# Pairs of heads that enter the shared buffers in three parts, with token-shift sums and chain steps issued later, in a streaming encoder layer on one core

## The chip, the cores and the metric

The kernel runs on one core of a Trainium2 chip. A core has a matrix engine (TensorE, PE in the profile; its weight loads are PEld), a vector engine (VectorE, DVE), a scalar engine (ScalarE, ACT), a general engine (GpSimd, POOL) and a sync engine (SyncE, SP), which here only issues DMAs. Each engine works through its own queue strictly in order, and engines wait for one another by semaphores. Matmuls write to PSUM, a small accumulator memory that DVE and ACT read and POOL does not; everything else lies in SBUF.

The metric is the device time of one execution in microseconds (us), as the median of several runs.

## The reference, cut to what matters

One layer: a projection of 1024 prompt rows and 64 sample rows, a gated-MLP half A and an RWKV-7 half B of 16 heads, and an output projection that sums both halves.

```python
z = h @ w_in                                     # (1024 + 64) x 2048 @ 2048 x 7296
za, zs, g_b = split(z)
u, v, g_a = split(za)
out_a = gelu(u) * sgu_mix(layer_norm(gelu(v)), w_s, b_s) * silu(g_a)

zs_mix = zs + mu * (previous_row(zs) - zs)       # token shift
r, k, vb, hw, ha = split(zs_mix)
decay = exp(-exp(-softplus(-(w0 + tanh(hw) @ w2)) - 0.5)); a = sigmoid(a0 + ha @ a2)
kk = normalise(k * k_k); k = k * (1 + (a - 1) * k_a)
for t in range(T):                               # per head, state S is 64 x 64
    S = S * w_t + (-S @ kk_t) (kk_t * a_t)^T + v_t k_t^T
    y_t = S @ r_t
y = group_norm(y) + (sum(r * k * r_k)) * v
out_b = y * silu(g_b)
o = concat([out_a, out_b]) @ w_out
y_out = rms_norm(x + o)
```

## The kernel before

**Order of the work.** The program is written by a planner in Python (class `Builder`): it emits instructions in one fixed order for each engine and keeps rough clocks (`self.clk`) only to decide what to emit next. The main line in `run` goes through the 57 blocks of `w_in` (128 columns each), then through `w_out` in two halves of eight weight groups (half 0 multiplies the first eight 128-row pieces of the concatenation, half 1 the others). A block of the projection is three groups of tokens (364, 364, 360); each group is 48 matmuls into one of two PSUM tiles `mp`. Values are split into two float16 parts, so each product takes three matmuls. After every second matmul the main line calls `poll`, which lets the generators in `self.side` emit a piece of other work when the time that they yielded has come on PE's clock.

**Side work.** Each weight block is prepared by `wprep` (ACT squares and casts, DVE forms the low part `w<-raw,sci,w`). Blocks 24 to 48 are token-shifted by `z_mix`: ACT evicts `mp` (and one last column, `zc` or `sht`), then DVE adds the shifted part straight from PSUM (`u<-mp,zs,u`).

**Pairs.** The 16 heads of half B go in eight pairs, each cut into 17 chunks of 64 rows (chunk 16 is the sample). `front(q)` makes the inputs of pair q; its elementwise products of 128x1088 run on POOL (`tt` with `eng=nc.gpsimd`). Then it copies them into the shared buffers `AR` and `KB`, in parts given by `PARTS`; a part of pair q may enter when pair q-1 has passed a flag (`mid` after chunk 7, `chain` at its end). `wkv(q)` forms the chunk products, inverts 32x32 triangles by a forward substitution of 60 DVE instructions (`u<-u`, `u<-u,u`), and then runs the chain over the chunks: matmul `yps<-S,wk`, DVE add `wk<-yps,wk`, matmul `smp<-wk`, DVE update `S<-S,pc,smp`, and again. After each half step it yields the time at which the DVE result is planned to be ready, plus `slack`. PE is in order, so a chain matmul that comes before its DVE result is ready stops the main line behind it.

**PSUM.** Side work shares two tiles `bigp` and two `smp`. `room(tags)` yields until the planner thinks that the next tiles have been read; `lora`, `head_sums` and `post` take tiles without it.

**Between the projections.** `mix_prep(0)` casts the eight pieces of half 0 to two float16 parts (ACT `...,pwi 128x544`, then DVE `...,pwi,... 128x544`), after the flag `kbfree` of pair 7. Pieces go to free slots `u`, or, once the projection is through, to the freed buffer of h (`bigt`), from where `mix_move` takes them later. `acc_load` loads x into the accumulators of the output; group 0's load is issued by SP. `out_first` multiplies weight group 0 with pieces 0 to 5 of four row tiles, then 6 and 7, and `out_add` adds the result to x on DVE (`bigt<-mp,sc,bigt`), which frees the PSUM tile.

Of the kernel before, what the change touches and what calls it, by code (L numbers as in the profile page):

```python
# [39 lines left out]
TWO23 = 8388608.0  # L40
PARTS = ((0, 8), (8, 17))
RES = 2


class Builder:
# [101 lines left out]
    def add(self, gen, front=False, backlog=600):  # L147
        if front:
            self.side.insert(0, [0, gen, 1e9])
        else:  # L150
            self.side.append([0, gen, backlog])

    def poll(self):
        self.npoll += 1
        assert self.npoll < 60000, [(g.__name__, g.gi_frame.f_lineno) for _, g, _ in self.side]
        for it in list(self.side):
            if it[0] > self.now or self.clk[DV] > self.now + it[2]:
                continue
            try:
                w = next(it[1])  # L160
                it[0] = self.now + 400 if w is None else w
            except StopIteration:
                self.side.remove(it)
# [30 lines left out]

    def tt(self, out, a, b, op, eng=None, dep=None):
        (eng or self.nc.vector).tensor_tensor(out, a, b, op)  # L196
        if eng is not None:
            return self.fin(PO, 100 + self.width(out) * 2.2, dep)
        return self.read(a, self.fin(DV, 150 + self.width(out) / 0.96, dep))
# [362 lines left out]
    def in_group(self, blk, st, t0, n):  # L562
# [25 lines left out]
        if 24 <= blk < 49:  # L588
            self.zmix = self.z_mix(blk, ps, t0, n, inv)
            self.evt = next(self.zmix)  # L590
            self.add(self.zmix, front=True)
            return
        else:
            o, func = self.U(self.gelu_buf[blk])[:, t0:t0 + n], AF.Gelu if blk < 16 else AF.Silu
            if blk in self.late:
                func = AF.Copy
        self.evt = self.act(o, ps[:, 0:n], func, scale=inv)

    def z_mix(self, blk, ps, t0, n, inv):
        i, g = blk - 24, MG.index((t0, n))  # L600
        o, zs, zc = self.U(self.gelu_buf[blk]), self.zs[:, self.zi % 2], self.zc[:, self.zi % 2]
        last = g == 2
        m = NP - t0 if last else n
        f = self.act(o[:, t0:t0 + n], ps[:, 0:n], AF.Copy, scale=zs[:, 0:1])
        c = self.sh[:, 0, i:i + 1] if last else zc[:, g:g + 1]
        f = self.act(c, ps[:, m - 1:m], AF.Copy, scale=inv)
        if last:
            f = self.act(self.sh[:, 1, i:i + 1], ps[:, n - 1:n], AF.Copy, scale=inv)
        yield f
        f = self.stt(o[:, t0 + 1:t0 + m], ps[:, 0:m - 1], zs[:, 1:2], o[:, t0 + 1:t0 + m], ALU.mult, ALU.add)  # L610
        if g:
            f = self.stt(o[:, t0:t0 + 1], zc[:, g - 1:g], self.vcol(V_MU, i), o[:, t0:t0 + 1], ALU.mult, ALU.add)
        if last:
            self.stt(o[:, NP + 1:NT], ps[:, m:n - 1], zs[:, 1:2], o[:, NP + 1:NT], ALU.mult, ALU.add)
            f = self.tt(o[:, NP:NP + 1], o[:, NP:NP + 1], self.mst[:, i:i + 1], ALU.add)
            self.flags.add(("zm", blk))
        yield f
# [175 lines left out]
    def lora(self, half, hw, out, bias):  # L793
        for t0, n in TG:
            pt = self.bigt()
            for p in range(2):
# [5 lines left out]
    def head_sums(self, a, b=None):  # L802
        b = a if b is None else b
        pa, pb, ps = self.bigt(), self.bigt(), self.smt()
        for h in range(2):
            hp, br, one = HP[h], HP[1 - h], self.bones[HP[h], HP[h]]
            self.mm(pa[hp, :], one, a[hp, 0:512], cost=260)
            self.mm(pb[br, :], one, a[hp, 512:1024], cost=260)
        for hp in HP:
            self.mm(ps[hp, 0:64], self.bones[hp, hp], a[hp, NP:NT], cost=55)  # L810
        parts = [(slice(0, 128), slice(0, 512), pa[:])] + [(HP[h], slice(512, 1024), pb[HP[1 - h]]) for h in range(2)]
        parts.append((slice(0, 128), slice(NP, NT), ps[:, 0:64]))
        return [(a[p, c], i) if b is a else (a[p, c], i, b[p, c]) for p, c, i in parts]

    def front(self, q):
# [41 lines left out]
        yield self.act(SQ, K, AF.Square, scale=self.vcol(V_KK, q))  # L857
        for o, i in self.head_sums(SQ):
            f = self.act(o, i, AF.Ln)
        yield f - 300  # L860
# [25 lines left out]
        for part, (c0, c1) in enumerate(PARTS):  # L886
            if q > 0:
                yield from self.wait(("mid" if part == 0 else "chain", q - 1))
            if part == 0:
# [12 lines left out]
        yield from self.wait(("vt", q))  # L902
        for _, i, o in self.head_sums(R, V):
            f = self.tt(o, i, o, ALU.mult)
        yield f
# [6 lines left out]
    def wkv(self, q):  # L912
# [5 lines left out]
        pc = self.pc[q % 2]  # L918
        slack = 250 if q < 7 else 0
        mv = MK.rearrange("p (r c) g k -> p c r g k", r=2)  # L920
        KR, BR = HP, (HP[1], HP[0])
        def vtr(part):
            c0, c1 = PARTS[part]
            V = self.U(P["v"])
            for c in range(c0, c1, 8):
# [12 lines left out]
                yield f  # L938
            if part:
                self.flags.add(("vt", q))  # L940
        af = AR.rearrange("p c s t -> p c (s t)")
        def ktr(part):
            c0, c1 = PARTS[part]
            if part:
                yield from self.wait(("kt0", q))
            for c in range(c0, c1, 4):
# [6 lines left out]
                yield f  # L953
            self.flags.add(("kbfree" if part else "kt0", q))
        def atr():
# [140 lines left out]
        for c in [16] + list(range(16)):  # L1096
# [22 lines left out]
            if c == 16:  # L1119
                yield from self.room("big")  # L1120
                pt = self.bigt()
                for h, hp in enumerate(HP):
                    self.mm(pt[0:64, hp], MR[:, c, h, :], VS[:, c, hp], cost=60)
                self.tt(yd, pt[0:64, 0:128], yd, ALU.add)
            elif c % 8 == 7:
                yield from self.room("big")
                pt = self.bigt()
                for i in range(4):
                    for h, hp in enumerate(HP):
                        for d in range(2):  # L1130
                            cc = c - 7 + 2 * i + d
                            self.mm(pt[HP[d], i * 128 + h * 64:i * 128 + h * 64 + 64], MR[:, cc, h, :], VS[:, cc, hp],
                                    cost=60)
                y = Y[:, c // 2 - 3:c // 2 + 1, :]
                self.tt(y, pt[:].rearrange("p (i f) -> p i f", f=128), y, ALU.add)
            if c == 16:
# [5 lines left out]
            else:  # L1142
                S = Sn
            if c == PARTS[0][1] - 1:
                self.flags.add(("mid", q))
            yield f + slack
# [31 lines left out]
    def post(self, q):  # L1178
# [15 lines left out]
        gg = self.vcol(V_GG, q)  # L1194
        for i in (0, 4):
            pt = self.bigt()
            for r in range(4):
                self.tr(pt[:, r * 128:(r + 1) * 128], YN[:, i + r].rearrange("p h f -> p (h f)"))
            c = slice(i * 128, i * 128 + 512)
            yield self.stt(BV[:, c], pt[:], gg, BV[:, c], ALU.mult, ALU.add)  # L1200
        pt = self.bigt()
        yield from self.wait(("yns", q))
        self.tr(pt[:, 0:64], self.yns[HP[q % 2]], 64, HP[q % 2])
# [185 lines left out]
    def acc_load(self):  # L1389
        nc = self.nc  # L1390
        self.accs = self.big[:, 16384:17408].rearrange("p (j t) -> p j t", t=64)
        for g in range(8):
            if g == 1:
                yield from self.wait(("mixT", 0))
            if g >= 4:
                yield from self.wait("moved")
            self.dma(nc.gpsimd if g else nc.sync, self.acc_view(g),
                     self.a["x"][0:NP, g * 256:(g + 1) * 256].rearrange("(t p) n -> p t n", p=128))
# [226 lines left out]
```

## Time and profile before

| | |
|---|---|
| median of 3 runs | 2029.97 us (2026.56 to 2030.69) |
| the profiled execution's own time | 2022.13 us |
| its span, first to last instruction | 2020.4 us |
| busy PE, DVE, ACT, POOL | 96%, 57%, 51%, 17% of the span |
| mean granted TensorE clock | 0.993 of full speed |

How to read it: PE is busy nearly all the time, so what can be won lies in the moments in which it is idle or runs at the lower clock, and each of them has a line and a cause in the trace. The profiled execution is 7.84 us (0.4%) below the median of the runs.

### The profile page before, as it was taken

What the parts mean: (1) busy time and instruction counts of PE and PEld (TensorE: products, weight loads), DVE (VectorE), ACT (ScalarE), POOL (GpSimd) and SP (SyncE); (2) the same over time, 40 slices, a digit from 0 to 9 for tenths busy, and PEclk for the clock granted to TensorE, in tenths of its full rate; (3) what the DMA queues carried; (4) which work ended last, traced back from release to release, by engine and by line L of the source; (5) the groups of instructions that cost most, each with busy time, mean ns of one, the idle gap of its engine ahead of it and who ended that gap; (6) DMA issues with size and microseconds to landing.
All of it is one profiled execution on the core that took longest, in us unless ns stands there. A gap on an engine that the chain in (4) does not pass through costs nothing.

```text
span 2020.4 us, 42834 instructions
## 1 busy us (share of the span) xinstructions
PE 1930.4 (96%) x18445; PEld 1393.1 (69%) x18445; DVE 1151.7 (57%) x2517; ACT 1026.6 (51%) x1834; POOL 339.7 (17%) x304
## 2 busy tenths in 40 slices
PE   6999999997999999899999989999999979999998
PEld 5966667665666666566666666666666658899997
DVE  6574684483475556647457565654754856533444
ACT  7633345555457455645655736755654542422433
POOL 2400002400410230240042022024004201000000
PEclk9999999999999999999999999999999989999999
DMA  6211124221212311322222222223122454412214
GB/s 234 95 64 42 66 81 158 92 66 60 89 61 96 110 62 54 108 105 70 88 90 67 99 94 74 88 76 118 39 98 99 151 191 130 167 43 89 80 34 146
DMA packets 52189, 190.65 MB, mean 94 GB/s; under 512 B 6880, under 2 KB 18672, under 8 KB 42336
## 3 DMA queue, kind: packets, MB, share of 16 engines
q1 hardware_dynamic: 42672, 156.71, 22.3%
q0 software_dynamic: 6880, 22.26, 3.2%
q10 hardware_dynamic: 2448, 8.94, 1.1%
q8 instruction: 145, 2.38, 0.5%
q14 instruction: 44, 0.36, 0.1%
HBM read 140.32 MB, written 45.93 MB: 92 GB/s over the span
## 4 chain that ended last, share of the span: by engine, by line
PE 82%; ACT 7%; DVE 7%; DMA 2%; issue 2%; SPq 0%; DVEq 0%; POOL 0%; ACTq 0%
PE mp L238 69%; PE bigp L238 7%; ACT u L184 3%; PE smp L238 2%; DVE w L192 2%; DVE u L192 2%; ACT L184 2%; PE bigp L243 1%; DVE u L196 1%; PE yps L238 1%; ACT w L184 1%; ACT wk L184 1%; DMA o_ss<-S 1%; DVE wk L196 1%; DVE S L1113 1%
## 5 line engine op out<-in xcount | busy, mean ns | idle before, releaser
L238 PE MATMUL mp<-bigt,w 128*128 128x364 f16 (+3 forms) x8514 | 1326.5, 310 | 4.3 <-DVE w L192 1.4
L238 PEld LDWEIGHTS <-w 128*128 128x128 f16 x9216 | 814.7, 98 | 410.2 <-issue 4.9
L192 DVE SCALAR_TENSOR_TENSOR w<-raw,sci,w 128x512 f16<-128x512 f32 x276 | 225.3, 841 | 186.8 <-ACT w L184 185.8
L238 PEld LDWEIGHTS <-wk 128*128 128x128 f16 x2304 | 210.4, 98 | 33.7 <-issue 10.2
L238 PE MATMUL mp<-w,wk 128*128 128x256 f16 x1728 | 204.3, 274 | 10.0 <-DVE bigt L192 10.0
L184 ACT ACTIVATE w<-raw,sci 128x512 f16<-128x512 f32 x276 | 186.3, 713 | 53.6 <-DVE sci L296 43.7
L196 POOL TENSOR_TENSOR u<-u,u 128x1088 f32<-128x1088 f32 x56 | 140.8, 2525 | 337.7 <-DVE u L192 129.1
L184 ACT ACTIVATE w<-raw 128x2048 bf16<-128x2048 f32 (+1 forms) x70 | 131.7, 1882 | 92.2 <-PE mp L238 85.9
L184 ACT ACTIVATE wk<-bigp 128x512 f32<-128x512 f32 (+5 forms) x240 | 120.1, 523 | 88.6 <-PE bigp L238 69.4
L184 ACT ACTIVATE u<-yps 64x128 f32<-64x128 f32 x120 | 32.7, 273 | 225.7 <-DVE wk L196 225.3
L184 ACT ACTIVATE u<-mp,sc 128x364 f32<-128x364 f32 (+3 forms) x109 | 57.0, 523 | 169.3 <-PE mp L238 168.7
L184 ACT ACT_TABLE_LOAD x95 | 121.9, 1283 | 35.0 <-PE bigp L238 19.1
L238 PE MATMUL mp<-w,u 128*128 128x256 f16 x1065 | 133.8, 276 | 3.4 <-DVE u L1039 2.9
L192 DVE SCALAR_TENSOR_TENSOR bigt<-mp,sc,bigt 128x512 f32<-128x512 f32 (+2 forms) x83 | 53.9, 652 | 130.5 <-PE mp L238 120.3
L238 PEld LDWEIGHTS <-u 128*128 128x128 f16 x1065 | 104.4, 99 | 18.6 <-DVE u L192 3.2
L196 POOL TENSOR_TENSOR wk<-wk,mask 128x512 f32<-128x512 f32 (+1 forms) x80 | 85.0, 1083 | 119.9 <-ACT wk L184 119.9
L1113 DVE SCALAR_TENSOR_TENSOR S<-S,pc,smp 64x64 f32<-64x64 f32 x240 | 66.8, 278 | 60.7 <-PE smp L238 52.5
L196 DVE TENSOR_TENSOR u<-u,u 128x30 f32<-128x30 f32 (+15 forms) x248 | 92.3, 372 | 8.3
L196 DVE TENSOR_TENSOR u<-bigp,u 128x512 f32<-128x512 f32 (+2 forms) x64 | 40.4, 632 | 92.1 <-PE bigp L238 90.8
L184 ACT ACTIVATE u<-mp,zs 128x364 f32<-128x364 f32 (+1 forms) x75 | 42.1, 561 | 96.1 <-PE mp L238 95.4
L192 DVE SCALAR_TENSOR_TENSOR u<-mp,zs,u 128x363 f32<-128x363 f32 (+1 forms) x100 | 49.5, 495 | 72.0 <-ACT zc L184 38.8
L238 PE MATMUL smp<-wk 64*64 64x64 f32 (+1 forms) x816 | 66.0, 239 | 21.4 <-DVE wk L196 19.9
(186 smaller groups left out, 1892.1 us busy)
## 6 DMA issues: line engine op xcount, KB each, us to landing
raw<-w_in SPq DMA_DIRECT2D x54, 1024.0 KB, 4.9
raw<-w_out SPq DMA_DIRECT2D x14, 1024.0 KB, 5.0
z_d<-u SPq DMA_DIRECT2D x24, 544.0 KB, 2.9
u<-z_d SPq DMA_DIRECT2D x24, 544.0 KB, 5.0
mix_d<-u ACTq DMA_DIRECT2D x16, 544.0 KB, 3.5
o_y<-bigt SPq DMA_DIRECT2D x16, 512.0 KB, 4.5
wk<-x SPq DMA_DIRECT2D x7, 1024.0 KB, 8.1
bigt<-x POOLq DMA_DIRECT2D x7, 1024.0 KB, 6.5
```

The source lines that it names most:

```text
L184: self.nc.scalar.activation(out, in_, func, bias=bias, scale=scale, **kw)
L192: self.nc.vector.scalar_tensor_tensor(out, in0, s, in1, op0, op1)
L196: (eng or self.nc.vector).tensor_tensor(out, a, b, op)
L238: self.nc.tensor.matmul(out, lhsT, rhs, start=start, stop=stop)
L243: self.nc.tensor.transpose(out, in_, self.ident[p, p])
L1113: self.nc.vector.scalar_tensor_tensor(Sn[hp, hp], Sc[hp, hp], pc[hp, c - 1:c], pu[hp, hp], ALU.mult, ALU.add)
```

## The change

Seven edits, of which the first six move instructions:

1. `PARTS` has three entries (chunks 0 to 7, 8 to 11, 12 to 16); the second may enter after chunk 11 of the pair before (flag `late`). The output sums of the chunks are made after chunks 7, 11 and 15, and those of chunk 16 by one 128x128 matmul and two adds in place of two matmuls and one add.
2. `z_mix` yields 800 ns more than the planned end of its eviction, and is put into `self.side` with that time, so that the sums are not emitted at the next poll but 800 ns after the planned eviction.
3. `slack` of the chain is 500 ns (250 before), still 0 for pair 7.
4. POOL's 128x1088 products are issued as two instructions.
5. `lora`, `head_sums` and `post` wait with `room` for tiles that are planned to have been read.
6. The load of x for group 0 is issued by ACT, not SP.
7. `HARD` in `poll` changes nothing (`w + 0`).

```diff
-PARTS = ((0, 8), (8, 17))
+PARTS = ((0, 8), (8, 12), (12, 17))
...
     def tt(self, out, a, b, op, eng=None, dep=None):
+        if eng is not None and self.width(out) == NT:
+            h = out.shape[1] // 2
+            for c in (slice(0, h), slice(h, out.shape[1])):
+                eng.tensor_tensor(out[:, c], a[:, c], b[:, c], op)
+            return self.fin(PO, 200 + NT * 2.2, dep)
...
             self.zmix = self.z_mix(blk, ps, t0, n, inv)
             self.evt = next(self.zmix)
-            self.add(self.zmix, front=True)
+            self.side.insert(0, [self.evt, self.zmix, 1e9])
...
-        yield f
+        yield f + 800
         f = self.stt(o[:, t0 + 1:t0 + m], ps[:, 0:m - 1], zs[:, 1:2], o[:, t0 + 1:t0 + m], ALU.mult, ALU.add)
...
     def lora(self, half, hw, out, bias):
         for t0, n in TG:
+            yield from self.room("big")
             pt = self.bigt()
...
+        yield from self.room("big", "big", "sm")
         pa, pb, ps = self.bigt(), self.bigt(), self.smt()
...
-                yield from self.wait(("mid" if part == 0 else "chain", q - 1))
+                yield from self.wait((("mid", "late", "chain")[part], q - 1))
...
-        slack = 250 if q < 7 else 0
+        slack = 500 if q < 7 else 0
...
-            elif c % 8 == 7:
+            elif c in (7, 11, 15):
+                m = 8 if c == 7 else 4
...
         for i in (0, 4):
+            yield from self.room("big")
             pt = self.bigt()
...
+        yield from self.wait(("yns", q))
+        yield from self.room("big")
         pt = self.bigt()
-        yield from self.wait(("yns", q))
...
-            self.dma(nc.gpsimd if g else nc.sync, self.acc_view(g),
+            self.dma(nc.gpsimd if g else nc.scalar, self.acc_view(g),
```

**Place one: DVE at the 36th of the 100 sums that read `mp`,** in the chain of pair 1. Before (`yps` is the chain's product, `S` its state, `sci` and `sc` belong to a weight block, `gst` to the group norm):

```order
L1113 SCALAR_TENSOR_TENSOR S_110<-S_109,pc_107,smp 64x64 x2
L295 TENSOR_SCALAR sci_116<-smp 128x1
L296 TENSOR_SCALAR sci_116<-sci_116 128x1
L298 TENSOR_SCALAR sc_113<-sci_116,kin 128x1
L220 RECIPROCAL gst<-gst 128x16
L192 SCALAR_TENSOR_TENSOR u_83<-mp,zs,u_83 128x363
L196 TENSOR_TENSOR wk<-yps,wk 64x128
```

The same sum in the changed kernel:

```order
L305 TENSOR_SCALAR sc_113<-sci_116,kin 128x1
L194 SCALAR_TENSOR_TENSOR u_90<-mp,zs,u_90 128x363
L1178 TENSOR_REDUCE gst<-u_84 128x16
L211 TENSOR_SCALAR gst<-gst 128x16
L194 SCALAR_TENSOR_TENSOR w_79<-raw,sci_116,w_78 128x512
L203 TENSOR_TENSOR u_84<-u_84,gst 128x1024
L203 TENSOR_TENSOR wk<-yps,wk 64x128
```

Before, the sum stands directly ahead of a chain add; now other work lies between them, and the chain of the pair begins later beside the main line. Over the whole program 42 of the 100 sums stand directly ahead of a chain instruction before, and 10 in the changed kernel.

**Place two: ACT from the last group of the input projection on.** Before (the 128x360 row is the last eviction of the projection; `...,pwi 128x544` are casts of half 0, two for each piece; the four pieces ahead of these rows are cast already):

```order
L184 ACTIVATE u_92<-mp,sc_113 128x360
L184 ACTIVATE w_79,sc_119<-raw 128x2048
L184 ACTIVATE u_91<-bigt,pwi 128x544 x2
L184 ACTIVATE bigt<-bigt,pwi 128x544
L184 ACTIVATE w_78<-raw,sci_116 128x512
L184 ACTIVATE bigt<-bigt,pwi 128x544 x5
L184 ACTIVATE wk<-u_90 32x8x2x32
```

The changed kernel:

```order
L186 ACTIVATE wk<-u_81,pwi 128x544
L186 ACTIVATE u_85<-mp,sc_113 128x360
L186 ACTIVATE w_79,sc_119<-raw 128x2048
L186 ACTIVATE wk<-u_81,pwi 128x544
L186 ACTIVATE wk<-u_86,pwi 128x544 x2
L186 ACTIVATE bigt<-u_87,pwi 128x544 x2
L186 ACTIVATE bigt<-bigt,pwi 128x544 x10
L186 ACTIVATE w_78<-raw,sci_116 128x512 x4
L253 DMA bigt<-x 128x8x256
```

Eight casts come after the last eviction before, fifteen now; the load of x stands behind them on ACT. Before it stood on SP, behind two loads of weights:

```order
L246 DMA bv_d<-u_92 128x1088
L246 DMA raw<-w_out 128x2048 x2
L246 DMA bigt<-x 128x8x256
L246 DMA g_d<-u_92 128x1088
```

**Place three: DVE in the changed kernel at the same point.** `u_88` and `u_83` are the forward substitution of pair 7:

```order
L194 SCALAR_TENSOR_TENSOR wk<-u_86,pwi,wk 128x544
L194 SCALAR_TENSOR_TENSOR bigt<-u_87,pwi,bigt 128x544 x2
L203 TENSOR_TENSOR u_83<-u_88 128x168
L203 TENSOR_TENSOR u_88<-u_88,u_83 128x24x7
L203 TENSOR_TENSOR u_83<-u_88 128x184
L203 TENSOR_TENSOR u_88<-u_88,u_83 128x23x8
L194 SCALAR_TENSOR_TENSOR bigt<-bigt,pwi 128x544 x4
L203 TENSOR_TENSOR u_83<-u_88 128x198
L203 TENSOR_TENSOR u_88<-u_88,u_83 128x22x9
L203 TENSOR_TENSOR u_83<-u_88 128x210
L203 TENSOR_TENSOR u_88<-u_88,u_83 128x21x10
L194 SCALAR_TENSOR_TENSOR bigt<-bigt,pwi 128x544 x4
```

Before, DVE has finished the 60 instructions of that substitution when it comes to the casts that follow the projection; now the casts lie in the middle of it.

## Rows read from the trace of the kernel before

**Rows 1.** Busy time by stage; columns: us, then PE, PEld, DVE, ACT, POOL, granted clock, DMA.

```profile
440.00:1606.00 1166.00, 1120.65 (x10555) 749.41 (x10553) 679.10 (x1547) 665.23 (x1163) 246.71 (x198) 1.00 0.24 85
1606.00:1666.00 60.00, 41.93 (x584) 32.90 (x582) 36.36 (x79) 25.30 (x44) 7.63 (x12) 0.86 0.60 208
...
sum 2020.40, PE 1930.38 PEld 1393.08 DVE 1151.74 ACT 1026.61 POOL 339.73; mean PE 386.08 PEld 278.62 DVE 230.35 ACT 205.32 POOL 67.95
```

**Rows 2.** What PE waited for, whole span: us in total, times, longest.

```profile
PE smp L238 <- DVE wk L196: 19.9, 13, 3.1
PE yps L238 <- DVE S L1113: 13.6, 14, 3.3
```

**Rows 3.** Timeline, stalls behind token-shift sums: start, us, engine, instruction, [idle before <-releaser].

```profile
490.98 0.79 PE L238 MATMUL smp<-wk 128*128 128x128 f32 x2 [2.76 <-DVE wk L196]
...
651.24 0.60 DVE L192 SCALAR_TENSOR_TENSOR u<-mp,zs,u 128x363 f32<-128x363 f32 x1 [3.52 <-ACT zc L184]
...
652.21 0.49 PE L238 MATMUL smp<-wk 128*128 128x128 f32 x2 [3.09 <-DVE wk L196]
...
1483.94 0.49 PE L238 MATMUL smp<-wk 128*128 128x128 f32 x2 [0.97 <-DVE wk L196]
```

**Rows 4.** Groups by line and shape: busy us, mean ns of one, idle before it.

```profile
L184 ACT ACTIVATE w<-raw 128x2048 bf16<-128x2048 f32 x68 | 129.6, 1907 | 91.9 <-PE mp L238 85.9 <-DMA raw<-w_in 5.9
...
L184 ACT ACTIVATE wk<-u,pwi 128x544 f16<-128x544 f32 x20 | 13.5, 734 | 3.4 <-DVE pwi L289 3.4
...
L196 POOL TENSOR_TENSOR u<-u,u 128x1088 f32<-128x1088 f32 x56 | 140.8, 2525 | 337.7 <-DVE u L192 129.1 <-DVE u L206 70.1 <-ACT w L184 56.3
...
L196 POOL TENSOR_TENSOR wk<-wk,pc 128x512 f32<-128x512 f32 x24 | 26.3, 1097 | 0.0
...
L192 DVE SCALAR_TENSOR_TENSOR wk<-u,pwi,wk 128x544 f16<-128x544 f32 x20 | 15.1, 779 | 6.3 <-ACT wk L184 6.3
...
L196 DVE TENSOR_TENSOR u<-u 128x240 f32<-128x240 f32 x16 | 6.5, 405 | 0.4
...
L192 DVE SCALAR_TENSOR_TENSOR w<-u,sci,w 128x512 f16<-128x512 f32 x8 | 5.6, 745 | 0.9 <-ACT w L184 0.9
```

**Rows 5.** Timeline, stalls while POOL runs its products.

```profile
503.19 0.49 PE L238 MATMUL smp<-wk 128*128 128x128 f32 x2 [1.14 <-DVE wk L196]
...
845.73 7.64 POOL L196 TENSOR_TENSOR u<-u,u 128x1088 f32<-128x1088 f32 x3 [1.50 <-DVE u L206]
...
849.04 4.88 DVE L192 SCALAR_TENSOR_TENSOR w<-raw,sci,w 128x512 f16<-128x512 f32 x2
...
854.28 0.49 PE L238 MATMUL smp<-wk 128*128 128x128 f32 x2 [2.59 <-DVE wk L196]
...
1504.37 0.49 PE L238 MATMUL yps<-S,wk 128*128 128x128 f32 x2 [0.57 <-DVE S L1113]
```

**Rows 6.** Timeline, a matmul that waits for its PSUM tile.

```profile
463.44 1.01 PE L238 MATMUL bigp<-u,lwh 128*128 128x512 f16 x2 [3.20 <-ACT wk L184]
```

**Rows 7.** The chain that ended last: a weight group of the output, start, us.

```profile
1747.73 22.38 PE mp L238 x240
```

**Rows 8.** Busy time and granted clock around the first pair's chain, columns as in rows 1.

```profile
454.50:505.00 50.50, 40.23 (x390) 26.49 (x391) 17.96 (x54) 27.83 (x51) 3.79 (x4) 0.93 0.17 60
```

**Rows 9.** Timeline from the last projection group to the second weight group of half 0.

```profile
1602.96 27.39 SPq L246 DMA_DIRECT2D raw<-w_out  x2
...
1610.66 0.32 PE L238 MATMUL mp<-bigt,w 128*128 128x360 f16 x1
...
1630.44 0.39 SPq L246 DMA_DIRECT2D bigt<-x  x1
...
1640.95 1.41 DVE L192 SCALAR_TENSOR_TENSOR bigt<-mp,sc,bigt 128x512 f32<-128x512 f32 x2 [9.76 <-DMA bigt<-x]
1641.75 1.44 PE L238 MATMUL mp<-w,wk 128*128 128x256 f16 x6 [7.76 <-DVE bigt L192]
...
1661.31 0.91 PE L238 MATMUL mp<-w,wk 128*128 128x256 f16 x4 [2.19 <-DVE bigt L192]
```

More of the change, by code (lines that the diff above doesn't have):

```diff
@@ L151, in add @@
             self.side.append([0, gen, backlog])
+    HARD = ("wkv", "startup")
     def poll(self):
@@ L160, in poll @@
                 w = next(it[1])
-                it[0] = self.now + 400 if w is None else w
+                it[0] = self.now + 400 if w is None else w if it[1].__name__ in self.HARD else w + 0
             except StopIteration:
@@ L806, in head_sums @@
             hp, br, one = HP[h], HP[1 - h], self.bones[HP[h], HP[h]]
-            self.mm(pa[hp, :], one, a[hp, 0:512], cost=260)
-            self.mm(pb[br, :], one, a[hp, 512:1024], cost=260)
+            self.mm(pa[hp, :], one, a[hp, 0:512], cost=230)
+            self.mm(pb[br, :], one, a[hp, 512:1024], cost=230)
         for hp in HP:
@@ L812, in head_sums @@
         parts.append((slice(0, 128), slice(NP, NT), ps[:, 0:64]))
-        return [(a[p, c], i) if b is a else (a[p, c], i, b[p, c]) for p, c, i in parts]
+        for p, c, i in parts:
+            yield a[p, c], i, b[p, c]
     def front(self, q):
@@ L857, in front @@
         yield self.act(SQ, K, AF.Square, scale=self.vcol(V_KK, q))
-        for o, i in self.head_sums(SQ):
-            f = self.act(o, i, AF.Ln)
+        for hs in self.head_sums(SQ):
+            if isinstance(hs, tuple):
+                f = self.act(hs[0], hs[1], AF.Ln)
+            else:
+                yield hs
         yield f - 300
@@ L902, in front @@
         yield from self.wait(("vt", q))
-        for _, i, o in self.head_sums(R, V):
-            f = self.tt(o, i, o, ALU.mult)
+        for hs in self.head_sums(R, V):
+            if isinstance(hs, tuple):
+                f = self.tt(hs[2], hs[1], hs[2], ALU.mult)
+            else:
+                yield hs
         yield f
@@ L938, in vtr @@
                 yield f
-            if part:
+            if part == 2:
                 self.flags.add(("vt", q))
@@ L944, in ktr @@
             if part:
-                yield from self.wait(("kt0", q))
+                yield from self.wait(("kt", q, part - 1))
             for c in range(c0, c1, 4):
@@ L953, in ktr @@
                 yield f
-            self.flags.add(("kbfree" if part else "kt0", q))
+            self.flags.add(("kt", q, part))
+            if part == 2:
+                self.flags.add(("kbfree", q))
         def atr():
@@ L1121, in wkv @@
                 pt = self.bigt()
-                for h, hp in enumerate(HP):
-                    self.mm(pt[0:64, hp], MR[:, c, h, :], VS[:, c, hp], cost=60)
-                self.tt(yd, pt[0:64, 0:128], yd, ALU.add)
-            elif c % 8 == 7:
+                self.mm(pt[:, 0:128], MR[:, c].rearrange("p g k -> p (g k)"), VS[:, c])
+                for hp in HP:
+                    self.tt(yd[:, hp], pt[hp, hp], yd[:, hp], ALU.add)
+            elif c in (7, 11, 15):
+                m = 8 if c == 7 else 4
                 yield from self.room("big")
                 pt = self.bigt()
-                for i in range(4):
+                for i in range(m // 2):
                     for h, hp in enumerate(HP):
                         for d in range(2):
-                            cc = c - 7 + 2 * i + d
+                            cc = c + 1 - m + 2 * i + d
                             self.mm(pt[HP[d], i * 128 + h * 64:i * 128 + h * 64 + 64], MR[:, cc, h, :], VS[:, cc, hp],
                                     cost=60)
-                y = Y[:, c // 2 - 3:c // 2 + 1, :]
-                self.tt(y, pt[:].rearrange("p (i f) -> p i f", f=128), y, ALU.add)
+                y = Y[:, (c + 1 - m) // 2:c // 2 + 1, :]
+                self.tt(y, pt[:, 0:m * 64].rearrange("p (i f) -> p i f", f=128), y, ALU.add)
             if c == 16:
@@ L1143, in wkv @@
                 S = Sn
-            if c == PARTS[0][1] - 1:
-                self.flags.add(("mid", q))
+            if c in (7, 11):
+                self.flags.add(("mid" if c == 7 else "late", q))
             yield f + slack
```

## Prediction

> **What bounds the kernel now.** I read first the busy times. PE works 1930.4 of the 2020.4 us span [rows 1], so 90 us of idle time, and the stretches in which its clock is low, are all that an edit of order can win. The busy time by stage says where they lie. The pairs' chains run beside the projection from 440 to 1606 us; there PE idles 1166.0 - 1120.65 = 45.35 us. The passage from the input to the output projection, 1606 to 1666 us, idles 18.07 us, at a granted clock of 0.86 of full speed [rows 1]. The remaining 27 us lie in the start and in the output stage, where the change moves nothing.
>
> Next come PE's waits. The two steps of the chain, `smp` waiting for DVE's add and `yps` waiting for DVE's state update, are 27 stalls and 33.5 us [rows 2], three quarters of the first figure. The length of each chain step is no trouble: a chain add takes some 0.28 us. So the timeline must tell why DVE is late. It shows two reasons, and a third that has to do with PSUM:
>
> - **Shift sums.** At 651.24 DVE has stood idle for 3.52 us at a token-shift sum whose input ACT has not yet evicted; the chain add is queued behind it, and PE stalls 3.09 us [rows 3]. Going through every stall, I count 10 that end behind such a sum, from 490.98 to 1483.94 us, 15.4 us in all.
> - **POOL.** Its 128x1088 products take 2.5 us each [rows 4]. While three of them run (845.73, 7.64 us), two DVE low parts take 4.88 us, where 0.745 us apiece is usual [rows 4, 5]; the chain step behind them comes 2.59 us late. I count 12 stalls of this kind, from 503.19 to 1504.37 us, 16.8 us in all.
> - **PSUM.** A product of `lora` waits 3.20 us for its tile, which ACT is still reading [rows 6]. With two smaller ones that is 5.2 us.
>
> What is left of the 45.35 us is 7.9 us in short pieces.
>
> **The change, part by part.** *The sums, 800 ns later and no longer at the head of the queue.* They are emitted when their eviction should be over, so DVE need not stand at them, and a chain add need not stand behind. Place one shows it: 42 of 100 sums stood directly ahead of a chain instruction, 10 do now. In proportion, 15.4 x 10/42 = 3.7 us stay; with the larger slack (next) I take 2. Bounds: nothing left, or half left (7.7) if the planner's time for the eviction is as far off as in [rows 3]. Gain 13.4 (7.7 to 15.4).
>
> *Slack 500 for 250 ns.* Each chain matmul is put a quarter of a microsecond further from its DVE result. It costs PE nothing, since projection matmuls fill the distance. The chains end later beside the main line: two half steps by 17 chunks by 0.25 = 8.5 us a pair, so far covered, because the next pair now enters by thirds; pair 7 has no slack in either kernel. From the short stalls it takes 0.25 us at best each; I put 7.9 at 6.5 afterwards, gain 1.4 (0 to 4).
>
> *POOL's products in halves.* The half does the same elements; by the 128x512 row it takes about 1.1 to 1.2 us [rows 4]. 56 more instructions cost POOL at most some microseconds, and POOL is 17% busy. If DVE gets its turn between the halves, what it can be held up at one time falls from 2.5 to 1.25 us. 12 stalls of 1.4 us on average become some of 0.6 at most, less 0.25 of slack: 4 us left. Bounds: if DVE does not get in between halves, as it hardly did between the three whole products [rows 5], slack alone takes 12 x 0.25 = 3 off 16.8; if it always gets in, 2.5 stay. Gain 12.8 (3 to 14.3), value near the upper end because the two low parts in [rows 5] did end while POOL had products to do.
>
> The Trainium skill ("SBUF — State Buffer", section "Who interferes with whom") says that a DVE instruction with two SBUF inputs and a GpSimd instruction reading SBUF share a port pair, which whoever issues first holds for its whole instruction, while DVE with one SBUF input is left alone. The 4.88 us in [rows 5] agrees. By that rule a DVE instruction waits for at most one half, and 2.5 us would stay in place of 4: the sum would come out 1.5 us lower.
>
> *Room.* `lora`, `head_sums` and `post` yield until their tiles are planned to be read; the matmuls of the projection go on meanwhile. Of 5.2 us I leave 0.5 (0 to 3, should the plan be wrong by as much as for the sums). Gain 4.7 (2.2 to 5.2).
>
> *Three parts, sums after chunks 7, 11 and 15.* PE loses 8 small matmuls in the whole program; DVE, 57% busy, gets 40 more instructions, ACT (51%) some 22, each on time that is idle now, so nothing. What this edit adds is placement: a pair's copies, transposes and products spread along the chain of the pair before it. If DVE's queue has more of them just ahead of chain instructions, the stalls come back; that is a rival below. The last pair's data, needed in the second half of the output, arrive about a weight group (22.4 us [rows 7]) later; half 0 has eight groups, and I count the margin at over three, some 70 us.
>
> These terms sum to 13.4 + 1.4 + 12.8 + 4.7 = 32.3 us of 45.35, leaving 13.
>
> *Clock.* Around the first pair's chain, 454.5 to 505, the granted clock is 0.93 in the mean, and PE idles 10.3 of 50.5 us [rows 8]. At the two levels of 1.2 and 2.4 GHz that is 0.14 x 50.5 = 7.1 us at the lower one, where half the work is lost: 3.5 us. If the waits there go, so does most of it; I take 2.5 (0 to 3.5).
>
> *The passage.* T0 is the end of the last projection matmul, 1610.98 us [rows 9]. Before, x's load waits on SP behind two loads of weights (27.39 us of that queue), is issued at 1630.44, and the first output add starts at 1640.95, T0 + 30.0, after DVE waited 9.76 us for it; PE stalled 7.76. The second weight group starts at 1661.31, T0 + 50.3 [rows 9]. In the changed kernel x is loaded from ACT, behind (place two) a square of 1.9 us, 15 casts of 0.734, four weight casts of about 0.7 and an eviction: T0 + 16.3. With the 10.5 us that the transfer took before it lands at T0 + 27. But DVE has there (place three) a wait for the first low part's cast, behind ACT's eviction, square and cast, of some 3.4 us, 15 low parts of 0.78, four of the weights at 0.745, and some 32 substitution steps, about 0.38 us each (0.405 for 128x240 [rows 4]): 3.4 + 11.7 + 3 + 12.2 = 30.3. So the first add starts at T0 + 30.3, when DVE is through rather than when x is there: the load's gain of four microseconds is not used. What follows it took 1661.31 - 1640.95 = 20.4 us, of which about 5 were pair 7's matmuls, now later: second group at T0 + 45 to 46. The 5 to 7 us of pair 7's work come back later, as PE's time or more idle time, since its chain has no slack. Net I take 1.5 us of loss. Bounds: 10 better (the adds come when x lands, T0 + 27, and the wait at 1661.31 and part of the lower clock go too), 8 worse (all of pair 7's work comes back, with the casts late).
>
> **Sum.** 2022.13 - 32.3 - 2.5 + 1.5 = 1988.8 for an execution like the profiled one. The median of the runs shown is 0.39% above it; by the same ratio the forecast is **1996 us**, and a microsecond of gain is a microsecond. Adding the bounds one way and the other would give gains of 13 to 50; they will hardly all fall the same way, and I take 24 to 46.
>
> The Trainium skill ("DMA: Bandwidth & Descriptors", section "Issuing engines are not separate DMA queues") says that another issuing engine saves only the time of issuing. By that alone the move of x's load would be worth some 0.4 us. The 27.39 us that its issue stood behind on SP [rows 9] speak against that here; the sum gives the move nothing for DVE's sake.
>
> **Rivals.**
> *A, the forecast,* gain 24 to 46, 1982 to 2006 us: 0.62.
> *B, the passage pays.* Pair 7 runs later than before relative to the projection (place three), its chain without slack then lies in the output's first groups, where DVE has the adds as well and every late chain step stops the output. With 34 chain steps at a third of a microsecond, 12 us more. For it: the 18 us idle there already. Against: output groups are long, and DVE is less loaded there. Gain about 21: 2009 us, 2006 to 2018: 0.18.
> *C, chain stalls only move.* Halves change nothing (DVE does not get in), and the new pair's parts stand where the sums stood. Then only the sums' part and PSUM's are won, half of it spent again: gain about 10, 2020 us: 0.12, of which 0.10 is faster by over 0.2%.
> *D, slower.* The first output add is held up in DVE's queue by the substitution, whose own steps wait for pair 7's inputs, and with the PSUM tiles full PE stops. The chain stage's 32 us are spent once the second weight group starts later than about T0 + 46 + 32 = T0 + 78, which is 28 us later than before. With 16 us, 2012; with 40, 2038. For it speaks only the order; DVE's own work there adds up to 30 us, not 60: 0.05.
> *E, it doesn't do what it says.* The planner's clocks err by more than 800 ns (DVE waited 3.52 us at one sum [rows 3]), sums still meet chain adds and halves come in one piece: 2030, 0.03.
>
> **How the numbers follow.** A, B and most of C are faster: 0.90; E and a little of C within 0.2% (4 us, about what this kernel's measurement can tell from no change): 0.04; D and the rest slower: 0.06. The range leaves out no more than 2 in 10 if it holds A and B: from 1981 to 2018 us.
>
> **What would show it.** Right: the two chain waits of [rows 2] sum to less than 12 us; DVE never idles over 1 us at a sum with a chain add behind it; POOL's halves at 1.2 us and no DVE instruction stretched by more than 1.3; no `lora` wait of 3 us; the stretch with the chains idles about 13 us; the clock around the first chain near 1.0; first output add at T0 + 30, second group at T0 + 45. Wrong would make it: low parts still stretched as in [rows 5] (halves useless), chain stalls of pair 7 in the output's groups (B), or a first output add past T0 + 40 (D).

## The result and the profile after

The changed kernel takes 1997.77 us (median of 4 runs, 1993.85 to 1999.07) against 2030.33 us before: ratio 0.9849, 95% interval 0.9824 to 0.9874. In a second measurement (a1 below) it took 1995.64 us, ratio 0.9841 (0.9826 to 0.9855). The forecast was 1996 us in 1981 to 2018.

The profiled execution took 1999.07 us. Its span is 1997.4 us, of which PE is busy 1929.3: it idles 68.1 us, where it idled 90.0 [rows 1]. The busy times by stage, columns as in [rows 1]; the last projection matmul now ends at 1588.94, 22.04 us earlier, so both stages end that much earlier:

```profile
440.00:1584.00 1144.00, 1117.22 (x10476) 750.03 (x10474) 671.18 (x1577) 651.91 (x1169) 256.88 (x248) 0.99 0.25 86
1584.00:1644.00 60.00, 44.64 (x602) 34.45 (x603) 48.58 (x104) 25.96 (x44) 3.83 (x7) 0.86 0.55 198
```

The chain stage idles 26.78 us (45.35 before), the passage 15.36 (18.07). PE's waits, as in [rows 2]:

```profile
PE mp L245 <- DVE bigt L194: 12.7, 7, 3.1
PE smp L245 <- DVE wk L203: 8.5, 9, 2.2
...
PE smp L245 <- DVE pw L219: 6.2, 2, 3.6
PE bigp L250 <- ACT wk L186: 5.2, 1, 5.2
PE yps L245 <- DVE S L1131: 4.9, 7, 1.1
PE smp L245 <- issue: 4.1, 2, 3.4
```

The two chain waits are 13.4 us in 16 stalls; they were 33.5 in 27. The wait of `bigp` for 5.2 us is new. The timeline shows what is left in the chain stage, first token-shift sums (answers to [rows 3]):

```profile
652.08 0.41 ACT L186 ACTIVATE sht<-mp,sc 128x1 f32<-128x1 f32 x2
652.52 0.52 DVE L194 SCALAR_TENSOR_TENSOR u<-mp,zs,u 128x295 f32<-128x295 f32 x1 [2.66 <-ACT sht L186]
...
653.97 0.49 PE L245 MATMUL smp<-wk 128*128 128x128 f32 x2 [1.04 <-DVE wk L203]
...
1489.97 0.52 DVE L194 SCALAR_TENSOR_TENSOR u<-mp,zs,u 128x295 f32<-128x295 f32 x1 [3.15 <-ACT sht L186]
...
1491.02 0.35 PE L245 MATMUL smp<-pw,ones 128*128 128x1 bf16 x8 [2.63 <-DVE pw L219]
```

DVE still stands idle at a sum, 2.66 us, for ACT's eviction. Five such stalls of the chains are left, 6.2 us, all behind the third group of a block. The last two lines are a sixth stall behind a sum, 2.63 us: it hits not a chain step but a small product `smp<-pw,ones` of a weight block, so that it is not among the two chain waits. (The other 3.6 us of that row of PE's waits lie in the start, in both kernels.) Next a stall beside POOL, and the place at which the new wait arises (answer to [rows 5]):

```profile
1354.64 4.61 POOL L201 TENSOR_TENSOR u<-u,u 128x576 f32<-128x576 f32 x3
...
1357.03 2.77 DVE L194 SCALAR_TENSOR_TENSOR w<-raw,sci,w 128x512 f16<-128x512 f32 x2
...
1360.17 0.49 PE L245 MATMUL smp<-wk 128*128 128x128 f32 x2 [1.02 <-DVE wk L203]
...
1556.49 2.64 POOL L201 TENSOR_TENSOR u<-u,u 128x544 f32<-128x544 f32 x2
1556.68 9.47 DVE L194 SCALAR_TENSOR_TENSOR w<-raw,sci,w 128x512 f16<-128x512 f32 x1 [0.85 <-ACT w L186]
1559.10 2.27 POOL L203 TENSOR_TENSOR wk<-wk,mask 128x512 f32<-128x512 f32 x2
1561.33 1.04 POOL L203 TENSOR_TENSOR wk<-wk,pc 128x512 f32<-128x512 f32 x1
1562.33 2.26 POOL L203 TENSOR_TENSOR wk<-wk,mask 128x512 f32<-128x512 f32 x2
1564.56 1.03 POOL L203 TENSOR_TENSOR wk<-wk,pc 128x512 f32<-128x512 f32 x1
1566.07 0.21 DVE L219 COPY wk<-u 128x128 f32<-128x128 f32 x1
...
1569.93 1.12 PE L250 MATMUL bigp<-ident,wk 128*128 128x128 f32 x4 [5.19 <-ACT wk L186]
```

At 1357 two low parts take 2.77 us, 1.3 more than usual. At 1556.68 one low part takes 9.47 us: it ends when POOL has gone through eight instructions without a pause. ACT and then PE wait behind it. Last the passage (answers to [rows 9]):

```profile
1596.83 0.42 ACTq L253 DMA_DIRECT2D bigt<-x  x1
...
1617.74 0.74 DVE L194 SCALAR_TENSOR_TENSOR bigt<-mp,sc,bigt 128x512 f32<-128x512 f32 x1
1618.54 1.44 PE L245 MATMUL mp<-w,wk 128*128 128x256 f16 x6 [3.14 <-DVE bigt L194]
...
1632.72 0.83 PE L245 MATMUL mp<-w,wk 128*128 128x256 f16 x6 [0.55 <-DVE bigt L194]
```

With T0 = 1588.94, the first add starts at T0 + 28.8 (forecast 30.3), the second group at T0 + 43.8 (forecast 45 to 46).

### The profile page after: what moved, and what is told of

Same layout as the page of the kernel before. It is cut to its first block, busy times and chain, and to the rows that moved or that the text cites. A ratio compares the mean times of both kernels' runs of the same rounds, so it can differ in the third digit from the quotient of the medians.

```text
span 1997.4 us, 42939 instructions
## 1 busy us (share of the span) xinstructions
PE 1929.3 (97%) x18429; PEld 1395.4 (70%) x18429; DVE 1152.4 (58%) x2557; ACT 1017.8 (51%) x1855; POOL 351.9 (18%) x360
## 5 line engine op out<-in xcount | busy, mean ns | idle before, releaser
L194 DVE SCALAR_TENSOR_TENSOR w<-raw,sci,w 128x512 f16<-128x512 f32 x276 | 231.7, 863 | 179.3 <-ACT w L186 178.7
L201 POOL TENSOR_TENSOR u<-u,u 128x544 f32<-128x544 f32 (+1 forms) x112 | 152.1, 1387 | 274.1 <-DVE u L194 82.5
L186 ACT ACTIVATE wk<-bigp 128x512 f32<-128x512 f32 (+6 forms) x248 | 120.8, 511 | 69.7 <-PE bigp L245 37.3
L245 PE MATMUL mp<-w,u 128*128 128x256 f16 x1035 | 127.9, 273 | 0.0
L203 DVE TENSOR_TENSOR u<-u,u 128x228 f32<-128x228 f32 (+15 forms) x248 | 90.8, 367 | 8.3
L203 DVE TENSOR_TENSOR u<-bigp,u 128x512 f32<-128x512 f32 (+3 forms) x72 | 41.6, 579 | 80.8 <-PE smp L245 55.5
L223 DVE STREAM_TRANSPOSE wk<-u 32x256 f32<-32x256 f32 (+1 forms) x128 | 57.9, 453 | 45.4 <-ACT u L186 43.6
```

What stands on the lines that cost most here:

```text
L186: self.nc.scalar.activation(out, in_, func, bias=bias, scale=scale, **kw)
L194: self.nc.vector.scalar_tensor_tensor(out, in0, s, in1, op0, op1)
L201: eng.tensor_tensor(out[:, c], a[:, c], b[:, c], op)
L223: self.nc.vector.transpose(out, a)
L245: self.nc.tensor.matmul(out, lhsT, rhs, start=start, stop=stop)
```

## The experiments

The theory at first: each edit takes away the cause that it is named for. The rival: the order as a whole decides where chain steps fall, and the edits do little alone. All runs are against the kernel before. To compare stalls, one fixed rule sorts every chain wait over 0.2 us: *sum*, if in the 5 us ahead DVE idled over 0.8 us at a token-shift sum; else *POOL*, if a DVE instruction in the 6 us ahead was over 0.4 us longer than usual while POOL ran; else *rest*. (In the prediction, where I sorted by eye, some on the border fell otherwise: 15.4 and 16.8 us.)

```
run                                ratio (95%)             PE idle  sum         POOL        rest
before                             1                       90.0     13, 17.5    9, 13.8     5, 2.2
a1 changed, again                  0.9841 (.9826-.9855)    68.5      5,  6.2   10,  6.9     1, 0.2
a2 products whole                  0.9865 (.9846-.9883)    71.9      5,  6.2    9,  9.7     1, 0.6
a3 products in quarters            0.9836 (.9820-.9853)    66.9      5,  6.2    5,  4.2     1, 0.6
a4 sums really later               0.9758 (.9743-.9773)    57.1      0          6,  6.9     7, 3.0
b1 slack 250                       1.0046 (1.0030-1.0061)  98.6     11, 29.9   12, 15.0     7, 2.6
b2 two parts                       0.9885 (.9869-.9902)    75.2      8, 10.6    6,  5.2     3, 3.7
b3 no room                         0.9907 (.9886-.9928)    80.8      7, 13.6    4,  5.4     0
b4 before + slack 500              1.0033 (1.0021-1.0046)  90.3     11, 12.5   16, 25.7     2, 0.6
c1 a4 + slack 250                  0.9802 (.9786-.9818)    64.5      0         13,  9.6     5, 2.2
c2 before + sums really later      0.9947 (.9932-.9962)    87.9      0         17, 24.7     0
c3 x from SP                       0.9890 (.9868-.9912)    75.2      5,  6.2   10,  6.9     1, 0.2
c4 a4 + quarters + hold of pair 7  0.9747 (.9731-.9764)    53.7      0          5,  4.5     7, 3.2
```

(idle: of the profiled execution, us; then stalls and us of each kind.)

**The edit of `z_mix` has no effect.** Ahead of all runs: with this edit undone, the changed kernel's order on all five engines is the same, word for word. In both kernels `in_group` takes what is left of the sums before its first matmul, so that neither the list's place nor the 800 ns is ever asked:

```python
        if self.zmix is not None:
            for _ in self.zmix:
                pass
            self.zmix = None
```

No run undoes the new places of the output sums (a part of edit 1), nor the planned cost of a `head_sums` matmul, 230 ns for 260, which the list of edits does not name.

**a1, the changed kernel again.** No edit.

> The changed kernel unchanged, as the base for the others and as a test of what repeats. If the stalls come from the order of the instructions, PE is idle for the same 68 us (within 2), in the same places, the 9.47 us low part beside POOL's products of the last pair included; only the clock differs, and with it the time by up to 5 us. If the long low part is chance, it is under 2 us here. Ratio to the kernel before 0.985.

The stalls of the chains repeat within 0.1 us; only waits for nothing that the profile shows ("issue") and a few in the passage differ more, by up to 0.7. The long low part is there again, 8.7 us over its usual length (in a2 8.6, in a3 9.0, in c3 8.7). It is order, not chance.

**a2, a3, the halves.** In a2 as below; in a3 four slices in place of two.

```diff
-            h = out.shape[1] // 2
-            for c in (slice(0, h), slice(h, out.shape[1])):
-                eng.tensor_tensor(out[:, c], a[:, c], b[:, c], op)
+            eng.tensor_tensor(out, a, b, op)
```

> Undoes one edit: POOL's 128x1088 products are one instruction again; the order on every other engine is the same, word for word. If the halves earn what the prediction gave them (12.8 us less 3 for the slack), the chain waits rise from 13.4 to some 21 to 23 us and the ratio is 0.989 to 0.990. If the stalls went because the chain's instructions stand elsewhere now (slack, parts), the waits rise by under 3 us and the ratio stays at 0.985 to 0.987. The lockout of 9.47 us stays in both.

> POOL's 128x1088 products in four instructions, nothing else moved. If DVE gets its turn after each POOL instruction, what it is held up at one time falls from about 1.0 to 0.5 us, the eleven stalls of the changed kernel beside POOL go from 7.2 to 3 or 4 us, and the ratio is lower by 0.001 to 0.002. If DVE gets in only where POOL pauses, stalls and time stay as they are or grow by POOL's longer total.

With the order fixed, whole products cost 3.4 us more idle time than halves and quarters save 1.6. POOL's stalls go 9.7, 6.9, 4.2. So DVE does get in between pieces, mostly, and the halves earn about a quarter of what the prediction gave them: with whole products in the new order the stalls beside POOL are 9.7 us, not the 13.8 of the kernel before. Not always: in b2 (below) three low parts of 3.47 to 3.57 us end only after both halves of a product. The medians say 6 us for a2 and nothing measurable for a3. A half takes 1.38 us in the mean, not 1.1 to 1.2:

```profile
L201 POOL TENSOR_TENSOR u<-u,u 128x544 f32<-128x544 f32 x80 | 108.6, 1382 | 261.4 <-DVE u L194 82.5 <-PE yps L245 57.7 <-PE mp L245 42.2
```

**a4, sums really later.** The lines quoted above move to the end of the next group, just ahead of the next `z_mix`.

> The token-shift sums really wait: the main line takes what is left of them at the end of the next group and not at its start, so that the 800 ns and the place in the list of side work take effect. In the changed kernel they have no effect (its order is the same without the edit, word for word). If the five stalls that are left behind sums (6.2 us, all at third groups) come from this, they fall to 1 to 2 us and the ratio is lower by 0.002. If ACT's eviction is late for the chain in any case, or the sums land on other chain steps, nothing or up to 3 us of loss.

All stalls behind sums are gone, and the time falls by 17 us, four times what I expected. But a4 does not measure the sums alone: the order of the rest moved too, and the long low part went with it (the longest takes 1.90 us). Of the idle time go 6.2 us of the chains, the 2.63 us of the sixth stall and the 5.2 us behind the long low part, and 4.6 us come in at the projection; with smaller shifts the net is 11.4. PE's waits:

```profile
PE yps L245 <- DVE S L1135: 8.9, 10, 2.4
...
PE mp L245 <- DVE bigt L194: 6.0, 6, 1.8
PE mp L245 <- DVE u L194: 4.6, 4, 1.5
PE mp L245 <- ACT wk L186: 4.3, 1, 4.3
```

The third row is the price: a projection matmul waits four times for its tile, which a late sum still reads.

**b1, b4, c1, the slack.** `slack = 250` for 500 in the changed kernel; 500 for 250 in the kernel before; and 250 on top of a4.

> Undoes one edit of the changed kernel: slack of the chain 250 ns again. If the larger distance is what keeps the chain from waiting for DVE (the sums still stand at the start of each group, and DVE is late by the same amounts), the chain waits rise from 13.3 us by 0.25 us for each stall that there is or that comes to light, to 20 to 25 us, and the ratio is 0.988 to 0.991. If place in the main line decides (three parts), waits stay under 17 us and the ratio at 0.984 to 0.986.

> The kernel before with one edit alone: slack 500 ns. If the distance does most of it, the chain waits fall from 33.5 to 18 to 22 us and the ratio is 0.992 to 0.994. If each edit only removes its own cause, as the prediction has it, they fall by at most 27 x 0.25 = 6.8 us, so to 27 us or more, and the ratio is 0.996 or more.

> The sums really later, as in a4, and the slack 250 ns as in b1. If what the slack earned in b1 (40 us) was distance from DVE as such, the kernel loses most of it again: chain waits over 30 us, ratio 0.99 or more. If the slack only moved chain steps off the sums at the group starts, the 29.9 us behind sums are gone here, chain waits are 12 to 20 us, and the ratio is 0.977 to 0.984.

Both expectations for b1 were wrong by far: without the larger slack the other edits are worse than nothing (40 us against a1). One of its stalls:

```profile
1342.08 0.25 ACT L186 ACTIVATE zc<-mp,sc 128x1 f32<-128x1 f32 x1
1342.37 0.59 DVE L194 SCALAR_TENSOR_TENSOR u<-mp,zs,u 128x363 f32<-128x363 f32 x1 [4.81 <-ACT zc L186]
1342.88 0.27 DVE L203 TENSOR_TENSOR wk<-yps,wk 64x128 f32<-64x128 f32 x1
...
1343.21 0.80 PE L245 MATMUL smp<-wk 128*128 128x128 f32 x2 [3.88 <-DVE wk L203]
```

The slack alone, on the kernel before, makes it 0.3% slower: stalls behind sums fall from 17.5 to 12.5, those beside POOL rise from 13.8 to 25.7. Other waits fall, and the idle time of its profile, 90.3 us, is that of before, so where the 0.3% arise is not shown. And with sums that do not block (c1), the slack is worth 9 us, not 40. So what it did in the changed kernel was in the main to put chain steps where no unready sum stands ahead of them, as c1's theory had it. Counting the first sum of each group, 28 of 75 stand ahead of a chain step before, with nothing but the group's own small sums between, 31 in b4, 20 in b1 and b3, 15 in b2, 6 in the changed kernel: slack, parts and room are each needed for it, and slack, the one of them that ran alone, does not bring it there.

**c2, sums later alone,** on the kernel before.

> The kernel before with this one edit alone, made so that it takes effect: the sums are left to the list of side work until the end of the next group. If the sums are a cause of their own, the 17.5 us of chain waits behind them fall to 0 to 2 us, idle time from 90 to some 75 us and the ratio to 0.989 to 0.993. If the chain steps then only meet POOL's products or other DVE work, waits beside POOL rise from 13.8 to over 25 us and the ratio is 0.997 or more.

Between the two: the 17.5 us behind sums go, 10.9 come back beside POOL's products (whole here), and the tile is waited for:

```profile
PE smp L238 <- DVE wk L196: 13.4, 6, 3.5
PE yps L238 <- DVE S L1117: 11.3, 11, 1.7
PE mp L238 <- DVE u L192: 10.1, 6, 2.2
```

**b2, b3, parts and room.** `PARTS = ((0, 8), (8, 17))` with the flags `mid` and `chain`; and the lines `yield from self.room(...)` of `lora`, `head_sums` and `post` taken out.

> Undoes one edit: two parts (chunks 0 to 7, 8 to 16) as before; the output sums after chunks 7, 11 and 15 stay. If the thirds spread the work of the next pair and so take stalls off the chain, the chain waits rise to 20 us or more and the ratio is 0.988 or more. If they only shift the last pair to a later place, the wait of 5.2 us beside POOL's products of the last pair goes, the passage is as before, and the ratio is 0.982 to 0.985.

> Undoes one edit: lora, head_sums and post take PSUM tiles without waiting for their readers. If the term was sized rightly (4.7 us), waits of PE at bigp for ACT come back, 4 to 6 us together, and the ratio is 0.986 to 0.987. If the order has moved so far that those places no longer meet, under 2 us of such waits and the ratio within 0.001 of 0.984.

b2 came out near the first of its two cases (chain waits 19.5 us, ratio 0.9885); b3's ratio lies above both of its cases, and its runs spread over 11 us. In b3 ACT waits at `bigp` come back (5.4 us, as sized). The larger loss of both lies in the passage, at a place that I had not thought of. In b3:

```profile
1622.09 1.11 ACT L186 ACTIVATE u<-u 128x1088 f32<-128x1088 f32 x1 [18.29 <-DVE u L203]
1622.14 0.33 ACTq L746 DMA_DIRECT2D mix_d<-u  x1
1622.49 0.53 ACTq L253 DMA_DIRECT2D bigt<-x  x1
...
1632.33 0.75 DVE L194 SCALAR_TENSOR_TENSOR bigt<-mp,sc,bigt 128x512 f32<-128x512 f32 x1 [5.68 <-DMA bigt<-x]
1633.13 1.23 PE L245 MATMUL mp<-w,wk 128*128 128x256 f16 x5 [19.71 <-DVE bigt L194]
```

The load of x stands on ACT behind a store that waits for DVE, and PE stalls 19.71 us. In b2 it is 12.47 us, behind the same kind of store. In the changed kernel this store is issued at 1567.63, ahead of the passage.

**c3, x from SP.** `nc.sync` for `nc.scalar` in `acc_load`.

> Undoes one edit of the changed kernel: x's first load is issued by SP again, all else in the same order. If the first output add waits for DVE's own queue (casts and the last pair's substitution), nothing changes: first add at 28.8 us after the last projection matmul within 0.5, ratio 0.983 to 0.986. If the load's place was what brought it forward, the add waits for x again, by 5 us or more, and the ratio is 0.987 or more.

```profile
1609.68 0.58 SPq L253 DMA_DIRECT2D bigt<-x  x1
...
1619.39 0.75 DVE L194 SCALAR_TENSOR_TENSOR bigt<-mp,sc,bigt 128x512 f32<-128x512 f32 x1 [7.24 <-DMA bigt<-x]
...
1620.19 1.44 PE L245 MATMUL mp<-w,wk 128*128 128x256 f16 x6 [10.56 <-DVE bigt L194]
```

The add waits 7.24 us for x again, PE stalls 10.56 (3.14 in the changed kernel), and some 10 us are lost, 6.7 of them as idle time. The second theory holds: in the new order SP issues the load at T0 + 26.4, ACT at T0 + 7.9.

**c4, an attempt at more.** a4 with quarters, and `if q == 7 and i >= 4: yield from self.wait(("mixT", 0))` in the forward substitution.

> An attempt at a faster version: sums later (a4), POOL's products in quarters (a3), and the last pair's substitution waits from its fourth step on until the casts of the first half are through. If the casts' low parts are late because the substitution stands between them on DVE, PE's waits for casts in the passage fall from some 13 to 6 us or less, waits beside POOL from 6.9 to 4, and the ratio is 0.970 to 0.974. If ACT's casts set the pace, or the last pair then comes late for the output's second half, the ratio is 0.975 or more.

The hold does what it says, but PE's waits for casts stay: `DVE bigt` 6.2, `ACT wk` 4.3 and `DVE wk` 3.7 us, against 6.0, 4.3 and 3.7 in a4. They lie at 1572 to 1585 us, and the held steps run from 1588 on. The 3.4 us less idle time are partly POOL's; the medians, 1976.63 and 1978.76, do not tell the two apart. Both beat the changed kernel by 17 to 19 us.

## Why the prediction was right, and where not

The time and the sign were right, and the place: the 45.35 us in the chain stage, chain steps late behind sums and POOL, are where most of the gain came from. Its sum for that stage was not, 32.3 us against 18.6, and most of the signs that it named for itself did not come: the chain waits are 13.4 us, not under 12, the stage idles 26.78, not 13, DVE still idles at sums, one DVE instruction is stretched by 8.7 us, and the clock around the first chain is 0.93. What came are the two times of the passage, and no `lora` wait of 3 us. By its own steps:

- *Sums, 13.4 us.* The step "they are emitted when their eviction should be over" is false. Chain stalls behind sums did fall, by 11.3 us, but because slack, parts and room together moved chain steps off them (b1 to b3). I counted 42 and 10 in the order and put it down to the nearest edit, without asking the order with that edit undone.
- *Slack, 1.4 us.* Mis-sized most: 40 us in its company (b1), 9 without blocking sums (c1), a loss of 0.3% alone (b4). I priced distance per stall; what it changes is which stalls there are.
- *Halves, 12.8 us.* The mechanism, one half at a time, is shown by a2 and a3 for most places; the size is 3.4 us of idle time. The rule of the Trainium skill ("SBUF — State Buffer", section "Who interferes with whom"), that whoever issues first holds the shared pair for its whole instruction while the other is blocked, agrees with all other DVE instructions of the changed kernel: none is over 1.2 us longer than usual, and a half takes 1.38. It does not explain the 9.47 us, through eight instructions, nor the 3.5 us in b2, through two.
- *Room, 4.7 us.* As sized for the waits it names (0.7 us left beside the one behind the long low part, 5.4 in b3); but without it 15 us are lost by the medians (b3), by way of the stall of 19.71 us in the passage above all. *Parts, nothing:* 7 us by b2, by 6.2 us more of chain waits and 9.3 more of PE's stall behind x's load, less other waits that went.
- *x's load, nothing.* Against the kernel before that was right: the first add is DVE's to time, T0 + 28.8. Against the changed order without the edit it is some 10 us (c3): I compared with the old queue, not with the one that the other edits make. The rule of the Trainium skill in "DMA: Bandwidth & Descriptors", section "Issuing engines are not separate DMA queues", that it saves only the time of issuing, falls short here by what stands ahead in SP's queue: 7.4 us of PE's stall in c3.
- *Passage.* Both times were met to about 2 us. I had a loss of 1.5; idle time fell by 2.7.
- *Clock, 2.5 us.* Not earned there. The waits around the first pair's chain did go (PE idles 3.8 us of the stretch of [rows 8], 10.3 before), but its granted clock is 0.93 again; "if the waits there go, so does most of it" was wrong.
- *Left out:* the long low part (5.2 us), the sixth stall behind a sum (2.6 us), and waits named "issue" (4.1 us), one of them at the first pair's chain.
- *Range.* The bounds as given add up to gains of 5 to 52 us, not 13 to 50 (the passage's 8 us of loss are missing in the sum), and a gain of 46 us is 1984 us, not 1982. Neither changes the forecast.

So the stage gave 18.6 of the 32.3 us, and the whole idle time 21.9. That the median still moved by 32.6 has two more parts. The first is the clock. The profiled execution of before had a mean granted clock of 0.993; seven others had 0.986 to 0.991, in the middle 0.988, and the changed kernel's eight 0.988 to 0.992, in the middle 0.990. At the same clock the two kernels lie some 27 to 29 us apart in all their runs: at 0.988 before took 2024.8 to 2027.5 us and the changed kernel 1998.8 and 1999.1, at 0.991 it is 2023.7 to 2024.5 against 1994.6 and 1995.1. So some 4 us of the 32.6 are the clock. The second part hides in PE's busy time. Before, and after:

```profile
393.48 1.14 PE L238 MATMUL bigp<-u,bones 64*64 64x512 f32 x5
393.96 0.14 PEld L238 LDWEIGHTS bigp<-u,bones 64*64 64x64 f32 x3 [0.30 <-ACT wk L184]
...
394.44 0.60 PE L238 MATMUL bigp<-u,bones 64*64 64x512 f32 x3
```

```profile
417.20 1.09 PE L245 MATMUL bigp<-u,bones 64*64 64x512 f32 x8
```

In nine of the 16 calls of `head_sums` before, a weight load in the middle waits for the `bigp` tile, eight times until ACT has read it and once until DVE has, while the matmul ahead of it still counts as busy. The eight matmuls take 1.57 or 1.63 us there in place of 1.09, 4.4 us in all; in the changed kernel no call does so. In b3, without `room`, it is one call of 16, so this is not in the main the work of `room`. The 2 us that remain are open. My conversion by 0.39%, from an execution with a high clock to the median, thus stood in for what the terms lacked: the time was near by luck, for the sum behind it was not right.

## What to carry to other kernels

Before a gain is put down to an edit that moves work to a later time, look for the place that forces the work out anyway, and compare the order with that one edit undone. In a program with one fixed order per engine edits do not add: the same 250 ns cost 0.3% alone and were worth 2% in company, because they choose which chain steps meet an unready instruction. Here it paid more to take the blocking away (17 us in a4, on top of the other edits; 10.6 alone, in c2) than to step around it. And a transfer's price is what stands ahead of it in the queue that it leaves and in the queue that it joins, in the new order.

## What was not expected of the hardware

One DVE low part was held for 9.47 us while POOL ran eight instructions back to back, though elsewhere DVE came in after one piece. It is so in five profiles, with about the same length: seven instructions and 9.30 us with whole products (a2), ten and 9.73 us with quarters (a3). What tells the two apart is open. And the load of x was issued by ACT at 1596.83, when the last eleven of the casts that stand ahead of it in ACT's order had not begun; they ran until 1603.9. The issue waited for its turn in the order, not for the work ahead to end.
